# Walking the columns of ring weights and accumulators in interleaved halves or quarters

## Chip, cores and metric

The kernel runs on 1 core of one Trainium2 chip. The metric is the device time in microseconds; two runs of the kernel before took 2642.73 and 2643.3 us.

## What is computed

Two transformer blocks over 256 tokens of width 2048, batch 1, all in float32. The first has gated linear attention, forgetting attention and memory attention behind one input projection, an output projection and a squared-ReLU MLP of width 8192; the second has sparse attention, a pooling mixer, cross attention and a gated feed-forward layer of width 5632. By far most of the arithmetic is in the projections, of which this is the pattern:

```python
def first_block(x, ...):
    h = x
    xn = rms_norm(h, attn_norm_g)
    proj = xn @ w_in
    ...
    h = h + (o * gate) @ w_out
    u = jax.nn.relu(rms_norm(h, mlp_norm_g) @ w_up)
    h = h + (u * u) @ w_down
    return h

def second_block(x, ...):
    ...
    y = (jax.nn.silu(h @ w_gate[l]) * (h @ w_up[l])) @ w_down[l]
    x = x + rms_norm_2(y, ln_ffn_post[l])
    return x
```

## The kernel before

Every projection is cut into groups of 512 output columns. A group has two accumulators, one PSUM bank of 128x512 float32 for each half of the 256 tokens (`gb`, four banks in turn). It walks the 2048 or more input features 128 at a time.

Float32 accuracy comes from a split in two. A weight tile arrives by DMA as `raw` (five buffers, 128x1024, that is two feature tiles of 512 columns). ScalarE copies it to `wh`, rounded to the type in which TensorE takes a four-byte word per column in one pass (float32r; line 133 is the helper for every activation), and VectorE subtracts that from `raw` to get the rest, `wl` (line 366). The activations are split the same way into `H` and `L`. Each product is then three matmuls into the same bank: H by wh (line 460), H by wl (line 461), L by wh (line 462). The activations are the stationary operand (128x128), the weights the moving one (512 columns).

The pairs (`wh`, `wl`) form a ring of six slots. `split` takes the next free slot from the front of `self.ring`, and `run_groups` appends it at the back when its unit of work is done, so the slots come round in order. A few units at special places hold their pair in other buffers and have no slot (`un.slot` is None); two projections of 20 and 48 columns are computed the other way round, with the weights stationary and 256 token columns moving (lines 450 to 452).

Everything else, attention, norms and transposes, is cut into small tasks that `pump` slips in between the matmuls of a unit; their matmuls go through lines 197 and 203. TensorE's order is thus fixed when the program is built.

The gated linear attention has one place in which VectorE walks an operand in short runs. For levels 1 to 7, with s = 128 >> level (64, 32, ... 1), it picks runs of s words out of every 2s words, in products (line 158) of levels 4 to 7 (s = 8, 4, 2, 1) and in a predicated copy (line 833):

```python
dst = st.rearrange("p (x b w s) -> p x b w s", x=8, w=2, s=s)[:, :, :, 1]
self.nc.vector.copy_predicated(dst, mk, b.rearrange("p (x b s) -> p x b s", x=8, s=s))
```

## Time and profile before

| | |
|---|---|
| median of 2 runs | 2643.02 us (2642.73 to 2643.3) |
| profiled execution | 2642.02 us |
| its span, first to last instruction | 2640.3 us |
| mean granted TensorE clock | 0.998 |
| TensorE busy | 2616.5 us (99%) |
| VectorE busy | 1504.9 us (57%) |
| ScalarE busy | 1251.9 us (47%) |
| HBM traffic | 190 GB/s over the span |

The profile is of one execution. Busy time of TensorE is made of matmul durations that overlap their neighbours; what a matmul costs is the distance between two starts. "Idle before" is the time that an engine stood still ahead of a group of instructions, with what ended it.

### The profile page before, as it was taken

Reading aid. Unit: us, or ns where it says so; the run is one execution under the profiler, and the core shown is the slowest. Engines: PE = TensorE matmul, PEld = TensorE weight load, DVE = VectorE, ACT = ScalarE, POOL = GpSimd, SP = SyncE. Lnnn points to the kernel's source line nnn. Section 1 sums busy time; section 2 is a strip of 40 time slices with the busy share of each in tenths; the row PEclk is TensorE's granted clock in tenths of the full one; section 3 lists DMA queues with packets and bytes.
Section 4 is the critical chain, followed back from the end, with each engine's and each line's share of the span. In section 5 each row is a group of like instructions: output and inputs, shape, how many; then the busy total and the mean of one; then the engine's idle time right before and its main releaser. Section 6 shows DMA issues by size and latency. Waiting matters only on the chain.

```text
span 2640.3 us, 32053 instructions
## 1 busy us (share of the span) xinstructions
PE 2616.5 (99%) x12196; PEld 2168.9 (82%) x12196; DVE 1504.9 (57%) x1921; ACT 1251.9 (47%) x1708; POOL 76.5 (3%) x97
## 2 busy tenths in 40 slices
PE   9999999999999999999999999999999999999998
PEld 7888888888888888888888888888788888888886
DVE  6567655555555555555566545666755455555555
ACT  7544544444444444444455344465554444444443
POOL 0001000000000000001000000000100000000001
PEclk9999999999999999999999999999999999999999
DMA  9643565555566565555444557555455555556553
GB/s 343 204 139 119 166 216 185 188 188 184 191 201 223 187 223 195 191 202 198 150 143 147 190 177 258 201 199 184 136 193 189 192 188 194 186 195 202 195 186 129
DMA packets 138891, 500.18 MB, mean 189 GB/s; under 512 B 15650, under 2 KB 16594, under 8 KB 138737
## 3 DMA queue, kind: packets, MB, share of 16 engines
q1 hardware_dynamic: 131760, 473.16, 53.0%
q0 software_dynamic: 6976, 24.98, 2.7%
q8 instruction: 95, 1.56, 0.2%
q14 instruction: 60, 0.48, 0.1%
HBM read 493.33 MB, written 7.88 MB: 190 GB/s over the span
## 4 chain that ended last, share of the span: by engine, by line
PE 94%; issue 4%; DVE 1%; ACT 0%; DMA 0%; POOL 0%; SPq 0%; DVEq 0%; ACTq 0%; POOLq 0%
PE gb L460 29%; PE gb L462 29%; PE gb L461 29%; PE pb L197 4%; PE pb L203 3%; DVE wl L366 0%; DVE s L169 0%; DMA s<-memT 0%; DVE s L158 0%; POOL st L232 0%; ACT wh L133 0%; PE gb L451 0%; ACT s L133 0%; PE gb L450 0%; PE gb L452 0%
## 5 line engine op out<-in xcount | busy, mean ns | idle before, releaser
L366 DVE TENSOR_TENSOR wl<-raw,wh 128x1024 fp32r<-128x1024 f32 (+1 forms) x876 | 1052.8, 1219 | 689.5 <-ACT wh L133 687.4
L460 PE MATMUL gb<-wh,s 128*128 128x512 f32 x3496 | 1383.9, 396 | 2.2 <-ACT wh L133 2.1
L461 PE MATMUL gb<-wl,s 128*128 128x512 f32 x3496 | 1362.5, 390 | 2.5 <-DVE wl L366 2.5
L462 PE MATMUL gb<-wh,s 128*128 128x512 f32 x3496 | 1363.4, 390 | 0.0
L133 ACT ACTIVATE wh<-raw 128x1024 fp32r<-128x1024 f32 (+1 forms) x878 | 914.0, 1055 | 802.2 <-PE gb L462 766.8
L462 PEld LDWEIGHTS gb<-wh,s 128*128 128x128 f32 x3496 | 656.4, 188 | 139.3 <-DVE s L169 0.5
L460 PEld LDWEIGHTS gb<-wh,s 128*128 128x128 f32 x3496 | 657.2, 188 | 137.4 <-ACT wh L133 3.7
L461 PEld LDWEIGHTS gb<-wl,s 128*128 128x128 f32 x3496 | 657.5, 188 | 135.1 <-DVE wl L366 4.2
L158 DVE TENSOR_TENSOR s<-gb,s 128x512 f32<-128x512 f32 x144 | 98.1, 691 | 159.6 <-PE gb L462 130.5
L133 ACT ACTIVATE s<-pb 128x512 fp32r<-128x512 f32 (+4 forms) x171 | 89.4, 536 | 163.6 <-PE pb L203 139.5
L133 ACT ACTIVATE s<-gb,st 128x512 f32<-128x512 f32 (+1 forms) x112 | 70.0, 642 | 199.5 <-PE gb L462 188.0
L197 PE MATMUL pb<-s,s 128*128 128x128 f32 (+4 forms) x720 | 116.5, 301 | 1.3 <-DVE s L158 0.9
L203 PE MATMUL pb<-cc,s 128*128 128x128 f32 x700 | 106.0, 274 | 5.4 <-DVE s L169 5.3
L203 PEld LDWEIGHTS pb<-cc,s 128*128 128x128 f32 x700 | 87.0, 141 | 29.0 <-DVE s L169 6.6
L197 PEld LDWEIGHTS pb<-s,s 128*128 128x128 f32 x720 | 97.7, 191 | 9.5 <-DVE s L158 1.3
L158 DVE TENSOR_TENSOR s<-pb,s 128x512 fp32r<-128x512 f32 (+4 forms) x87 | 57.5, 664 | 62.4 <-ACT s L133 58.6
L133 ACT ACTIVATE s<-pb,vecs 128x256 fp32r<-128x256 f32 (+2 forms) x109 | 42.3, 453 | 49.9 <-PE pb L203 40.5
L163 DVE TENSOR_SCALAR s<-gb,st 128x512 f32<-128x512 f32 (+1 forms) x32 | 20.9, 658 | 67.8 <-PE gb L462 51.5
L169 DVE SCALAR_TENSOR_TENSOR s<-pb,vecs,s 128x256 fp32r<-128x256 f32 (+1 forms) x104 | 40.0, 435 | 29.0 <-ACT s L133 29.0
L133 ACT ACTIVATE s<-s,st 128x128 f32<-128x128 f32 (+2 forms) x73 | 32.8, 450 | 31.7 <-DVE st L163 30.4
L133 ACT ACTIVATE s<-s 128x512 f32<-128x512 f32 (+3 forms) x46 | 37.0, 807 | 21.5 <-DVE s L158 12.4
L232 POOL TENSOR_TENSOR st<-st,nhalf 128x8 f32<-128x8 f32 (+2 forms) x21 | 26.1, 1243 | 689.5 <-DVE st L165 689.5
(113 smaller groups left out, 565.0 us busy)
## 6 DMA issues: line engine op xcount, KB each, us to landing
raw<-w_in SPq DMA_DIRECT2D x216, 512.0 KB, 4.2
raw<-w_up SPq DMA_DIRECT2D x216, 512.0 KB, 4.4
raw<-w_down SPq DMA_DIRECT2D x216, 512.0 KB, 4.4
raw<-w_gate SPq DMA_DIRECT2D x88, 512.0 KB, 4.6
raw<-w_out SPq DMA_DIRECT2D x32, 512.0 KB, 4.5
raw<-w_mix_out SPq DMA_DIRECT2D x32, 512.0 KB, 4.6
raw<-w_br_pool SPq DMA_DIRECT2D x16, 512.0 KB, 5.2
raw<-w_br_attn SPq DMA_DIRECT2D x16, 512.0 KB, 4.1
```

Source lines behind the costliest of these rows:

```text
L133: self.nc.scalar.activation(out, in_, func, **kw)
L158: self.nc.vector.tensor_tensor(out, a, b, op)
L163: self.nc.vector.tensor_scalar(out, a, s1, None, op0=op0)
L169: self.nc.vector.scalar_tensor_tensor(out, a, s, b, op0, op1)
L197: self.nc.tensor.matmul(out, lhsT, rhs, start=start, stop=stop)
L203: self.nc.tensor.transpose(out, in_, self.ident[:k, :k])
L232: self.nc.gpsimd.tensor_tensor(r, t, self.nhalf[:, :k], op=OP.pow)
L366: self.nc.vector.tensor_sub(l[:, :m], r, h[:, :m].bitcast(F32))
L460: mm(o, H[:, c:c + 128], wh, start=st, stop=False)
L461: mm(o, H[:, c:c + 128], wl, start=False, stop=False)
L462: mm(o, L[:, c:c + 128], wh, start=False, stop=sp)
```

## The change

By ring slot, the moving operand (`wh` or `wl`) and the accumulator are both seen through the same rearranged view. `(a, c)` cuts the 512 columns into `a` parts and takes `c` columns of each in turn: (2, 2) takes columns 0, 1, 256, 257, 2, 3, 258, 259 and so on. The values and where they are summed stay the same; the order within a matmul changes. Slot 0 and the units without a slot keep the plain order.

```diff
@@ -454,9 +454,16 @@
                     if k % 4 == 3 and not sp:
                         self.pump()
                     continue
+                PAT = {0: None, 1: (2, 2), 2: (2, 4), 3: (2, 32), 4: (4, 2), 5: (2, 16)}[un.slot or 0]
+                if PAT:
+                    a_, c_ = PAT
+                    perm = lambda z: z.rearrange("p (a b c) -> p b a c", a=a_, c=c_)
+                else:
+                    perm = lambda z: z
+                wh, wl = perm(wh), perm(wl)
                 for t in ts:
                     c = (kt % 4) * 256 + t * 128
-                    o = g.bk[t]["ap"]
+                    o = perm(g.bk[t]["ap"])
                     mm(o, H[:, c:c + 128], wh, start=st, stop=False)
                     mm(o, H[:, c:c + 128], wl, start=False, stop=False)
                     mm(o, L[:, c:c + 128], wh, start=False, stop=sp)
```

On TensorE, in the first group of the program, this stands before for the second token half with ring slot 1 and then for slots 2 and 3 (`wh1`, `wl1` are slot 1's pair, `gb0` and `gb1` the accumulators of the token halves, `s` the split activations; the last column is the moving shape):

```order
L460 MATMUL gb1_83<-wh1_72,s2_3_133 128x512
L461 MATMUL gb1_83<-wl1_73,s2_3_133 128x512
L462 MATMUL gb1_83<-wh1_72,s3_4_134 128x512
L460 MATMUL gb0_82<-wh2_74,s2_3_133 128x512
L461 MATMUL gb0_82<-wl2_75,s2_3_133 128x512
L462 MATMUL gb0_82<-wh2_74,s3_4_134 128x512
L460 MATMUL gb1_83<-wh2_74,s2_3_133 128x512
L461 MATMUL gb1_83<-wl2_75,s2_3_133 128x512
L462 MATMUL gb1_83<-wh2_74,s3_4_134 128x512
L460 MATMUL gb0_82<-wh3_76,s2_3_133 128x512
```

and at the same place after (the three lines are 467 to 469 now; the shape reads partitions, jumps, parts, run):

```order
L467 MATMUL gb1_83<-wh1_72,s2_3_133 128x128x2x2
L468 MATMUL gb1_83<-wl1_73,s2_3_133 128x128x2x2
L469 MATMUL gb1_83<-wh1_72,s3_4_134 128x128x2x2
L467 MATMUL gb0_82<-wh2_74,s2_3_133 128x64x2x4
L468 MATMUL gb0_82<-wl2_75,s2_3_133 128x64x2x4
L469 MATMUL gb0_82<-wh2_74,s3_4_134 128x64x2x4
L467 MATMUL gb1_83<-wh2_74,s2_3_133 128x64x2x4
L468 MATMUL gb1_83<-wl2_75,s2_3_133 128x64x2x4
L469 MATMUL gb1_83<-wh2_74,s3_4_134 128x64x2x4
L467 MATMUL gb0_82<-wh3_76,s2_3_133 128x8x2x32
```

No row has moved: the operands and their order are the same, and only the shape in which the 512 columns are walked differs. A little later in the same group, still on TensorE, this stands after where the work goes from slot 4 to slot 5 (before, the same rows with 128x512):

```order
L467 MATMUL gb1_83<-wh4_78,s6_7_183 128x64x4x2
L468 MATMUL gb1_83<-wl4_79,s6_7_183 128x64x4x2
L469 MATMUL gb1_83<-wh4_78,s7_8_184 128x64x4x2
L467 MATMUL gb0_82<-wh5_80,s6_7_183 128x16x2x16
L468 MATMUL gb0_82<-wl5_81,s6_7_183 128x16x2x16
L469 MATMUL gb0_82<-wh5_80,s7_8_184 128x16x2x16
```

Slot 4 walks four quarters in runs of 2, slot 5 two halves in runs of 16; again nothing has moved.

## Rows read from the trace of the kernel before

**Rows 1.** The page, span and busy time of each engine

```profile
span 2640.3 us, 32053 instructions
...
PE 2616.5 (99%) x12196; PEld 2168.9 (82%) x12196; DVE 1504.9 (57%) x1921; ACT 1251.9 (47%) x1708; POOL 76.5 (3%) x97
```

**Rows 2.** The page, the chain that ended last, by engine and by line

```profile
PE 94%; issue 4%; DVE 1%; ACT 0%; DMA 0%; POOL 0%; SPq 0%; DVEq 0%; ACTq 0%; POOLq 0%
PE gb L460 29%; PE gb L462 29%; PE gb L461 29%; PE pb L197 4%; PE pb L203 3%; DVE wl L366 0%; DVE s L169 0%; DMA s<-memT 0%; DVE s L158 0%; POOL st L232 0%; ACT wh L133 0%; PE gb L451 0%; ACT s L133 0%; PE gb L450 0%; PE gb L452 0%
```

**Rows 3.** The page, costliest groups: count | busy us, mean ns | idle us, releaser

```profile
L366 DVE TENSOR_TENSOR wl<-raw,wh 128x1024 fp32r<-128x1024 f32 (+1 forms) x876 | 1052.8, 1219 | 689.5 <-ACT wh L133 687.4
L460 PE MATMUL gb<-wh,s 128*128 128x512 f32 x3496 | 1383.9, 396 | 2.2 <-ACT wh L133 2.1
L461 PE MATMUL gb<-wl,s 128*128 128x512 f32 x3496 | 1362.5, 390 | 2.5 <-DVE wl L366 2.5
L462 PE MATMUL gb<-wh,s 128*128 128x512 f32 x3496 | 1363.4, 390 | 0.0
L133 ACT ACTIVATE wh<-raw 128x1024 fp32r<-128x1024 f32 (+1 forms) x878 | 914.0, 1055 | 802.2 <-PE gb L462 766.8
```

**Rows 4.** Timeline of TensorE from 1000 to 1004 us: start, duration in us

```profile
999.82 0.39 PE L460 MATMUL gb<-wh,s 128*128 128x512 f32 x1
1000.05 0.39 PE L461 MATMUL gb<-wl,s 128*128 128x512 f32 x1
1000.28 0.39 PE L462 MATMUL gb<-wh,s 128*128 128x512 f32 x1
...
1003.90 0.39 PE L460 MATMUL gb<-wh,s 128*128 128x512 f32 x1
```

**Rows 5.** Engines' busy time in three long stretches, with granted clock

```profile
core 0: us, PE busy (x) PEld busy (x) DVE busy (x) ACT busy (x) POOL busy (x), PEclk, DMA share, GB/s
...
8.00:100.00 92.00, 89.54 (x400) 72.97 (x400) 59.65 (x76) 64.55 (x111) 9.12 (x10) 1.00 0.88 323
100.00:1900.00 1800.00, 1793.90 (x8534) 1489.64 (x8531) 1054.61 (x1446) 868.41 (x1234) 53.91 (x69) 1.00 0.55 185
1900.00:2626.00 726.00, 723.15 (x3236) 598.97 (x3237) 378.96 (x383) 311.56 (x351) 10.78 (x10) 1.00 0.56 186
```

**Rows 6.** Timeline of TensorE, 99.5 to 107 us, the 20-column projection

```profile
99.74 0.28 PE L450 MATMUL gb<-s,wh 128*20 128x256 f32 x1
99.86 0.28 PE L451 MATMUL gb<-s,wl 128*20 128x256 f32 x1
99.97 0.28 PE L452 MATMUL gb<-s,wh 128*20 128x256 f32 x1
...
102.37 0.28 PE L452 MATMUL gb<-s,wh 128*20 128x256 f32 x1
```

**Rows 7.** Timeline of VectorE, 163 to 178 us, levels 1 to 7 in order

```profile
163.44 0.73 DVE L833 COPY_PREDICATED s<-lmask,pb 128x512 f32<-128x512 int32 x1 [0.87 <-PE pb L197]
164.07 1.17 DVE L158 TENSOR_TENSOR s<-s,s 128x256 f32<-128x256 f32 x3
165.64 0.74 DVE L833 COPY_PREDICATED s<-lmask,pb 128x512 f32<-128x512 int32 x1 [0.40 <-PE pb L197]
166.27 1.17 DVE L158 TENSOR_TENSOR s<-s,s 128x256 f32<-128x256 f32 x3
...
168.61 0.71 DVE L833 COPY_PREDICATED s<-lmask,pb 128x512 f32<-128x512 int32 x1
169.22 1.17 DVE L158 TENSOR_TENSOR s<-s,s 128x256 f32<-128x256 f32 x3
170.42 0.72 DVE L833 COPY_PREDICATED s<-lmask,pb 128x512 f32<-128x512 int32 x1
171.04 1.17 DVE L158 TENSOR_TENSOR s<-s,s 128x256 f32<-128x256 f32 x3
...
173.38 0.70 DVE L833 COPY_PREDICATED s<-lmask,pb 128x512 f32<-128x512 int32 x1
174.71 1.31 DVE L833 COPY_PREDICATED s<-lmask,pb 128x512 f32<-128x512 int32 x1 [0.63 <-PE pb L197]
...
176.99 1.30 DVE L833 COPY_PREDICATED s<-lmask,pb 128x512 f32<-128x512 int32 x1
```

## The prediction

> **What bounds the kernel now.** I read the engine totals first: TensorE is busy 2616.5 of 2640.3 us, the next engine, VectorE, 1504.9 [rows 1]. The chain that ended last confirms that it is the limit: 94% of it is TensorE, 29% on each of lines 460, 461 and 462 [rows 2]. The costliest groups give the counts: each of these three lines has 3496 matmuls of 512 columns against weights from the ring, 10488 in all, and they sat idle for only about 2 us each; the ScalarE split that feeds them was idle 802.2 us, 766.8 of it waiting for line 462, that is, for TensorE to let go of a ring slot [rows 3]. So a nanosecond on each of these matmuls is 10.5 us of the end, and nothing that the change does elsewhere can count.

> The mean duration in those rows (390 to 396 ns) is not the price of a matmul, since they overlap. The price is the distance from one start to the next: in a quiet stretch of the timeline 18 steps take 1003.90 - 999.82 = 4.08 us, 226.7 ns each [rows 4]. [...] It isn't a fixed cost of a matmul: those of 256 columns on lines 450 to 452, with only 20 columns of stationary operand to load, take 23 steps in 102.37 - 99.74 = 2.63 us, 114.3 ns each, again about 0.445 ns a column [rows 6]. [...]

> **What the change does.** No instruction is added, removed or moved: the same matmuls stand in the same order on TensorE, and the other engines' work is the same. Only the access patterns of lines 460 to 462 differ, by ring slot. The ring is first in, first out over six slots, so each slot has a sixth of the matmuls, about 1748. Slot 0 and the units outside the ring keep their order. Slots 1 to 5 walk weights and accumulator in runs of 2, 4, 32, 2 and 16 words, from two halves 1024 bytes apart (slots 1, 2, 3, 5) or four quarters 512 bytes apart (slot 4). No new wait appears; LDWEIGHTS, the splits and the transfers are untouched.

> What a run of two costs on TensorE this trace doesn't show: no matmul of it walks so. The nearest rows are on VectorE, in the gated linear attention, where one operand is walked in runs of 64, 32, ... 1 words with gaps of the same length. The predicated copy (line 833) of 512 words takes 0.73, 0.74, 0.71, 0.72 and 0.70 us for runs of 64, 32, 16, 8 and 4, and then 1.31 and 1.30 us for runs of 2 and 1 [rows 7]. Runs of 4 every 8 words cost nothing; runs of 2 every 4 words cost 1.87 times as much, and so do single words every 2: in both, 512 words lie spread over 256 aligned groups of four words, and in the earlier ones over 128. So what that operation pays for is groups of four touched, not words and not jumps. On the other side, three products on line 158 take 1.17 us together whether the runs are 8, 4, 2 or 1 [rows 7]: at VectorE's pace of about a word per nanosecond a pair per group is still no burden. TensorE asks for a word every 0.44 ns, more than twice that pace, and with pairs it would have to open a new group every 0.89 ns, twice as often as it does now.

> The sum, slot by slot:
> - Slots 2, 3 and 5 (runs of 4, 32, 16; all begin on a group's first word): still 128 groups for each matmul. I cost them at nothing, because runs of 4 and more are free in both VectorE rows. [...]
> - Slots 1 and 4 (runs of 2): every pair opens a group, and the other half of the group is fetched again later: 256 groups. [...] Upper bound: the predicated copy's extra 0.61 us for its 256 pairs, laid on each matmul as it stands. In between, 256 groups at TensorE's own 1.77 ns are 453.4 ns, and the copy's ratio of 1.87 gives 424 ns. I take 453.4, since it is priced by TensorE's own row, and 424 is near.
> - So 2 x 1748 = 3496 matmuls cost 226.7 ns more each: +792.5 us.
> - What the slower matmuls hide: TensorE stood idle for 2.5, 6.1 and 2.9 us in the three long stretches [rows 5], mostly on splits and transfers. Splits will now be ready earlier relative to TensorE, so up to some 11 us could go; I take 6.
> - Accumulators: they are walked in the same order, so sums land where they did. A write in pairs I cost at nothing more than the fetch, as the two go in step.

> The profiled execution took 2642.02 us (its span 2640.3), 1.0 below the median of 2643.02. From the median: 2643 + 792.5 - 6 = about 3429 us. With 424 ns in place of 453.4 it is 3327; with both halves of the cost a little dearer, up to 3530. Its own range is 3320 to 3530.

> [...]

> **The rivals.**
> - *Pairs are free* (ends at no change). If SBUF hands TensorE two adjacent words per access whatever the jump between accesses, all five orders run at 226.7 ns and the time stays at 2643. For it: line 158's 1.17 us with runs of 2 and 1, and every run in the change being even and aligned. Against it: the predicated copy, which doubled with the same runs. [...]
> - *Two groups can be held open.* Then the two halves of slot 1 share their fetches and are free, and only the four quarters of slot 4 pay: 1748 x 226.7 = 396 us, 3036 with 3 us hidden. A price for both slots well under double (say 50% more, 3496 x 113 = +395) ends at the same place. Nothing in the trace speaks for either beyond the two VectorE rows disagreeing.
> - *Every jump costs a group's time*, slot 2's included: three slots double, 5244 x 226.7 = +1189, about 3825; the upper bound of the pair price, 3496 x 0.61 = +2130, lies beyond. Against it: runs of 4 cost nothing in either row.
> [...]

> **How the numbers follow.** Forecast 0.48; pairs free 0.26; one slot or a part of the price 0.14; every jump dear 0.05; faster 0.07. The prediction is 3429 us. For 8 in 10 the range must hold the first three: 2635 to 3530, which leaves out 0.07 below and about 0.06 above. Slower by over 2% is 0.48 + 0.14 + 0.05 = 0.67, within 2% 0.26, faster by over 2% 0.07; 2% is about what a measurement of this kernel tells from no change.

> **What would show it.** In the profile after, the distances between starts of the three matmul lines should fall into two kinds by shape: about 453 ns for the shapes of 128x2x2 and 64x4x2, and 227 ns for all others. TensorE's busy share stays at 99%, ScalarE's and VectorE's fall to about 0.37 and 0.44 of the span, with their added idle time put down to line 462's successor. I am wrong if 128x2x2 runs at 227 (pairs free, or held open, according to what 64x4x2 does), if 64x2x4 is slower than 8x2x32, or if any shape comes under 220.

## The result and the profile after

The changed kernel took 3295.93 us (median of 2 runs, 3294.96 to 3296.89) against 2643.02: a ratio of 1.2471, 95% interval 1.2449 to 1.2492. It is slower by 653 us, where 786 were forecast, most of it in the two slots from which the forecast had its cost (table below). The profiled execution took 3294.96 us with a span of 3293.2, 652.9 more than before.

The page, span, engines and the chain that ended last, to be read beside [rows 1, 2]:

```profile
span 3293.2 us, 32051 instructions
...
PE 3274.3 (99%) x12196; PEld 2230.0 (68%) x12196; DVE 1510.1 (46%) x1921; ACT 1263.4 (38%) x1708; POOL 76.6 (2%) x97
...
PE 99%; DVE 0%; ACT 0%; DMA 0%; SPq 0%; issue 0%; POOL 0%; DVEq 0%; ACTq 0%
PE gb L467 31%; PE gb L468 31%; PE gb L469 31%; PE pb L197 3%; PE pb L203 2%; DMA s<-memT 0%; DVE wl L366 0%; DVE s L169 0%; ACT s L133 0%; PE gb L452 0%; PE gb L451 0%; PE gb L450 0%; ACT wh L133 0%; SPq L340 0%; SPq L208 0%
```

The number of matmuls is the same, 12196, VectorE's and ScalarE's work is the same to 1%, and TensorE alone has grown, by 658 us of busy time. The costliest groups, to be read beside [rows 3]:

```profile
L467 PE MATMUL gb<-wh,s 128*128 128x512 f32 x3496 | 1627.9, 466 | 1.4 <-ACT wh L133 1.3
L468 PE MATMUL gb<-wl,s 128*128 128x512 f32 x3496 | 1605.6, 459 | 1.2 <-DVE wl L366 1.2
L469 PE MATMUL gb<-wh,s 128*128 128x512 f32 x3496 | 1605.4, 459 | 0.0
L366 DVE TENSOR_TENSOR wl<-raw,wh 128x1024 fp32r<-128x1024 f32 (+1 forms) x876 | 1055.3, 1219 | 1055.7 <-ACT wh L133 1048.1
L133 ACT ACTIVATE wh<-raw 128x1024 fp32r<-128x1024 f32 (+1 forms) x878 | 922.5, 1063 | 1212.9 <-PE gb L469 1162.0
```

All three lines grew by 242 to 244 us of busy time, whichever operand they stream, and the split on ScalarE now waits 1162.0 us for line 469 where it waited 766.8 for line 462, the same matmul. A group of the profile mixes the six slots, so the price of an order has to be read from starts in the timeline. The first matmuls of six units in a row, on slots 1, 2, 3, 4, 5 and 0, each unit of 12 matmuls (start, duration in us):

```profile
1904.57 0.68 PE L467 MATMUL gb<-wh,s 128*128 128x512 f32 x1
...
1908.68 0.42 PE L467 MATMUL gb<-wh,s 128*128 128x512 f32 x1
...
1911.69 0.40 PE L467 MATMUL gb<-wh,s 128*128 128x512 f32 x1
...
1914.54 0.68 PE L467 MATMUL gb<-wh,s 128*128 128x512 f32 x1
...
1919.91 0.43 PE L467 MATMUL gb<-wh,s 128*128 128x512 f32 x1
...
1922.83 0.40 PE L467 MATMUL gb<-wh,s 128*128 128x512 f32 x1
...
1925.59 0.50 PE L467 MATMUL gb<-wh,s 128*128 128x512 f32 x1
```

A twelfth of each distance is 343, 251, 238, 448, 243 and 230 ns; before, all were at 227 [rows 4]. Over the whole trace, taking each matmul's start to the next matmul's start and sorting by the ring slot of its weights (the sums include what waits fell there):

| slot, order | matmuls | median ns, before | after | sum us, before | after | more | forecast |
|---|---|---|---|---|---|---|---|
| 0, plain | 1758 | 227 | 229 | 404.7 | 408.8 | 4.1 | 0 |
| 1, (2, 2) | 1746 | 227 | 340 | 407.0 | 597.8 | 190.8 | 396 |
| 2, (2, 4) | 1746 | 227 | 254 | 401.6 | 442.0 | 40.4 | 0 |
| 3, (2, 32) | 1746 | 227 | 236 | 403.9 | 418.6 | 14.7 | 0 |
| 4, (4, 2) | 1740 | 227 | 443 | 400.3 | 777.1 | 376.8 | 396 |
| 5, (2, 16) | 1752 | 227 | 240 | 403.8 | 429.5 | 25.7 | 0 |

The sum, 652.5 us, is the whole difference of the spans. Nothing went anywhere else.

### The profile page after: what moved, and what is told of

Read it like the earlier page. It is cut to its first block, busy times and chain, and to the rows that moved or that the text cites. A ratio compares the mean times of both kernels' runs of the same rounds, so it can differ in the third digit from the quotient of the medians.

```text
span 3293.2 us, 32051 instructions
## 1 busy us (share of the span) xinstructions
PE 3274.3 (99%) x12196; PEld 2230.0 (68%) x12196; DVE 1510.1 (46%) x1921; ACT 1263.4 (38%) x1708; POOL 76.6 (2%) x97
## 4 chain that ended last, share of the span: by engine, by line
PE 99%; DVE 0%; ACT 0%; DMA 0%; SPq 0%; issue 0%; POOL 0%; DVEq 0%; ACTq 0%
PE gb L467 31%; PE gb L468 31%; PE gb L469 31%; PE pb L197 3%; PE pb L203 2%; DMA s<-memT 0%; DVE wl L366 0%; DVE s L169 0%; ACT s L133 0%; PE gb L452 0%; PE gb L451 0%; PE gb L450 0%; ACT wh L133 0%; SPq L340 0%; SPq L208 0%
## 5 line engine op out<-in xcount | busy, mean ns | idle before, releaser
L467 PE MATMUL gb<-wh,s 128*128 128x512 f32 x3496 | 1627.9, 466 | 1.4 <-ACT wh L133 1.3
L468 PE MATMUL gb<-wl,s 128*128 128x512 f32 x3496 | 1605.6, 459 | 1.2 <-DVE wl L366 1.2
L469 PE MATMUL gb<-wh,s 128*128 128x512 f32 x3496 | 1605.4, 459 | 0.0
L133 ACT ACTIVATE wh<-raw 128x1024 fp32r<-128x1024 f32 (+1 forms) x878 | 922.5, 1063 | 1212.9 <-PE gb L469 1162.0
L469 PEld LDWEIGHTS gb<-wh,s 128*128 128x128 f32 x3496 | 676.4, 193 | 341.1 <-issue 143.2
L467 PEld LDWEIGHTS gb<-wh,s 128*128 128x128 f32 x3496 | 676.4, 193 | 322.0 <-issue 130.0
L468 PEld LDWEIGHTS gb<-wl,s 128*128 128x128 f32 x3496 | 676.2, 193 | 317.5 <-issue 127.4
L158 DVE TENSOR_TENSOR s<-gb,s 128x512 f32<-128x512 f32 x144 | 99.0, 691 | 267.5 <-PE gb L469 226.7
L203 PEld LDWEIGHTS pb<-cc,s 128*128 128x128 f32 x700 | 89.5, 144 | 44.3 <-issue 18.9
```

The lines of the kernel that those rows point to most:

```text
L133: self.nc.scalar.activation(out, in_, func, **kw)
L158: self.nc.vector.tensor_tensor(out, a, b, op)
L203: self.nc.tensor.transpose(out, in_, self.ident[:k, :k])
L467: mm(o, H[:, c:c + 128], wh, start=st, stop=False)
L468: mm(o, H[:, c:c + 128], wl, start=False, stop=False)
L469: mm(o, L[:, c:c + 128], wh, start=False, stop=sp)
```

## The experiments

Kernels for which one time is given ran once; the kernel before, run seven times beside the first four kernels below, took 2641.13 to 2643.95 us (median 2643.28). Each edit is against the changed kernel or, where said, against the kernel before. The three matmul lines shift by a few with each edit. Medians are of the distances from one start to the next, by slot, as in the table.

**Which side pays, the read or the write.** Two kernels, each with one half of the change: the first permutes only the weights, the second only the accumulators.

```diff
-                    o = perm(g.bk[t]["ap"])
+                    o = g.bk[t]["ap"]
```

> Only the weights are walked in the new orders, the accumulators plainly, so columns of slots 1 to 5 are summed into the wrong places (the values differ, the number and size of all instructions do not). SBUF theory (the moving read pays for groups of words that it opens): all of the cost is here, start distances of 340 ns (128x2x2) and 443 ns (64x4x2) as in the changed kernel, time 3280 to 3300 us. PSUM theory (the accumulator write pays): every matmul at 227 ns, time 2640 to 2650 us. Both pay and add up: a time between, 2800 to 3150 us, with the rest in the run that permutes the accumulators alone.

```diff
-                wh, wl = perm(wh), perm(wl)
```

> Only the accumulators are walked in the new orders, the weights plainly; the values land in other columns, the work is the same. SBUF theory: 2640 to 2650 us, 227 ns for all slots. PSUM theory: 3280 to 3300 us, with 340 and 443 ns. Both pay: between.

With the weights alone permuted the time was 3295.36 us, the changed kernel's within 0.6 us, and the medians by slot were 340, 254, 236, 443 and 240 ns, the same as in the table. With the accumulators alone it was 2643.74 us, the kernel before's (2643.28), and 227 ns in every slot. The first matmul line of the kernel that permutes the weights, to be read beside the changed kernel's:

```profile
L467 PE MATMUL gb<-wh,s 128*128 128x512 f32 x3496 | 1627.6, 466 | 2.1 <-ACT wh L133 2.1
```

The costliest groups of the kernel that permutes the accumulators, the same as [rows 3]:

```profile
L466 PE MATMUL gb<-wh,s 128*128 128x512 f32 x3496 | 1384.0, 396 | 2.8 <-ACT wh L133 2.7
L467 PE MATMUL gb<-wl,s 128*128 128x512 f32 x3496 | 1363.1, 390 | 2.6 <-DVE wl L366 2.5
L468 PE MATMUL gb<-wh,s 128*128 128x512 f32 x3496 | 1363.8, 390 | 0.0
```

So the whole cost is in reading the moving operand from SBUF; the order of the writes into PSUM cost nothing in any of the five patterns.

**The change without its pairs.** Slots 1 and 4 plain, the others as changed:

```diff
-                PAT = {0: None, 1: (2, 2), 2: (2, 4), 3: (2, 32), 4: (4, 2), 5: (2, 16)}[un.slot or 0]
+                PAT = {0: None, 1: None, 2: (2, 4), 3: (2, 32), 4: None, 5: (2, 16)}[un.slot or 0]
```

> Slots 1 and 4, which walked in runs of two, go back to the plain order; slots 2, 3 and 5 keep (2,4), (2,32) and (2,16). If each slot's matmuls pay for their own order alone, what is left is 39 + 16 + 25 us (the slot sums of the changed kernel less those of before): 2715 to 2730 us, 2.7 to 3.3% slower than before. Rival, as the prediction had it: runs of four and more are free, and their small extra in the changed kernel came from their neighbours in pairs: 2640 to 2655 us.

It took 2727.59 us (median of 4 runs) against 2643.28, a ratio of 1.0319 (1.0302 to 1.0336). Line 467 of its page:

```profile
L467 PE MATMUL gb<-wh,s 128*128 128x512 f32 x3496 | 1413.1, 404 | 2.0 <-ACT wh L133 1.9
```

Its sums by slot are 41 us more in slot 2, 16 in slot 3 and 22 in slot 5, much as in the changed kernel: 79 us for three slots, and 5 us more in slot 0, which has kept the plain order. Each order pays for itself, and the price of longer runs is real, where the prediction had nothing.

**More streams.** Weights and accumulators together, other numbers in slots 1 to 5:

```diff
-                PAT = {0: None, 1: (2, 2), 2: (2, 4), 3: (2, 32), 4: (4, 2), 5: (2, 16)}[un.slot or 0]
+                PAT = {0: None, 1: (8, 2), 2: (4, 4), 3: (8, 4), 4: (2, 8), 5: (4, 16)}[un.slot or 0]
```

> Weights and accumulators in the same order, with other numbers for slots 1 to 5: (8,2), (4,4), (8,4), (2,8), (4,16). Group theory (with more than two streams every pair opens its group of four words anew at some 1.73 ns, and runs of four are whole groups): (8,2) at 443 ns as (4,2); (4,4), (8,4), (2,8), (4,16) between 227 and 255 ns; time about 3120 us. Distance theory (what costs is the 512 bytes between quarters, less so the 1024 between halves): (8,2), with 256 bytes between its parts, is well away from 443 ns, and (4,4) is dearer than the 254 ns of (2,4), at 300 ns or more.

3295.73 us, where the group theory gave about 3120; that it is nearly the changed kernel's time is chance, since the slots differ. The medians were 487 ns for (8, 2), 269 for (4, 4), 278 for (8, 4), 244 for (2, 8) and 232 for (4, 16). This separates little: eight streams of pairs cost 10% more than the group theory's 443, (4, 4) lies above its 255, but not at the 300 of the distance theory. Distance and number of streams changed together here, so the next kernel parts them.

**Distance or streams.** Moving read alone, pairs, with the parts at chosen distances (against the kernel before; distances in words of four bytes):

```diff
+                W = {1: (2, 128), 2: (2, 512), 3: (2, 32), 4: (4, 256), 5: (4, 64)}.get(un.slot) if un.nkt == 2 else None
+                if W:
+                    m_, d_ = W
+
+                    def walk(z):
+                        return bass.AP(z.tensor, z.offset, [list(z.ap[0]), [2, 256 // m_], [d_, m_], [1, 2]])
+                    wh, wl = walk(h), walk(l)
```

> Moving read alone, pairs only, accumulators plain (the weights read are other columns, some twice, so the values differ; number and size of the instructions are the same). Two streams 512, 2048 and 128 bytes apart in slots 1, 2 and 3, four streams 1024 and 256 bytes apart in slots 4 and 5. Stream theory (the port can keep two groups open, not four): 340 ns in slots 1 to 3 and 443 ns in slots 4 and 5 whatever the distance, time about 3990 us. Distance theory (how far a jump goes sets its price, 512 bytes being dear and 1024 cheap): slot 1 at 443 ns or more, slot 4 at 340, slot 2 at 340 or less.

3968.61 us; medians 340, 340 and 327 ns for two streams, 443 and 443 for four. The timeline at the first matmuls of slots 2, 3, 4, 5 and 0, where four streams 1024 bytes apart (the third row to the fourth) take the same 5.32 us for twelve as four streams 256 bytes apart (the fourth row to the fifth):

```profile
2292.64 0.51 PE L467 MATMUL gb<-wh,s 128*128 128x512 f32 x1
...
2296.58 0.51 PE L467 MATMUL gb<-wh,s 128*128 128x512 f32 x1
...
2300.52 0.64 PE L467 MATMUL gb<-wh,s 128*128 128x512 f32 x1
...
2305.84 0.64 PE L467 MATMUL gb<-wh,s 128*128 128x512 f32 x1
...
2311.16 0.43 PE L467 MATMUL gb<-wh,s 128*128 128x512 f32 x1
```

The distance theory falls: for pairs in streams like these, what counts is how many streams are alternated, not how far apart they are.

**Groups opened, or jumps.** One ascending stream, moving read alone (against the kernel before); each list is [step, count], innermost last, and a step of 0 reads the same words again:

```diff
+                steps = {1: [[4, 256], [1, 2]], 2: [[2, 128], [0, 2], [1, 2]], 3: [[8, 128], [1, 4]],
+                         4: [[4, 64], [0, 2], [1, 4]], 5: [[16, 16], [0, 2], [1, 16]]}.get(un.slot) if un.nkt == 2 else None
+                if steps:
+                    walk = lambda z: bass.AP(z.tensor, z.offset, [list(z.ap[0])] + steps)
+                    wh, wl = walk(h), walk(l)
```

> Moving read alone, one ascending stream, accumulators plain (other columns are read, some twice; number and size of the instructions are the same). Slot 1: pairs every 4 words (256 groups of four, each opened once); slot 2: every pair read twice running (64 groups); slot 3: four words every 8 (128 groups); slot 4: every four words read twice running (64 groups); slot 5: every 16 words read twice running (64 groups, opened twice). [...] Jump theory (each access that does not follow on the last costs, whether or not its group is open): 340 ns in slots 1 and 2 alike, 227 to 255 in slots 3 and 4, 240 in slot 5.

3028.04 us. The first matmuls of slots 2, 3, 4, 5, 0 and 1 and of the unit behind:

```profile
1757.18 0.40 PE L465 MATMUL gb<-wh,s 128*128 128x512 f32 x1
...
1759.79 0.40 PE L465 MATMUL gb<-wh,s 128*128 128x512 f32 x1
...
1762.59 0.38 PE L465 MATMUL gb<-wh,s 128*128 128x512 f32 x1
...
1765.18 0.41 PE L465 MATMUL gb<-wh,s 128*128 128x512 f32 x1
...
1768.06 0.40 PE L465 MATMUL gb<-wh,s 128*128 128x512 f32 x1
...
1770.83 0.61 PE L465 MATMUL gb<-wh,s 128*128 128x512 f32 x1
...
1776.25 0.40 PE L465 MATMUL gb<-wh,s 128*128 128x512 f32 x1
```

A twelfth each: 218, 233, 216, 240, 231 and 452 ns; the medians over the trace are 216, 233, 216, 240, 231 and 452. Pairs that each open a new group cost 452; pairs that are each read twice running cost 216. The second walk has half as many jumps as the first (128 steps back for 255 steps on), so the two are not quite alike, but it is also faster than the plain order, which has none. The jump theory wanted 340 for both and falls; in slot 5 it had the right number, 240. The group theory (the price is the number of groups opened) holds: 256 groups at 1.77 ns are 453.4. And with only 64 groups to open, a matmul runs at 216 ns, below the 227 of the kernel before.

**Aligned groups, or length of run.** Moving read alone again (against the kernel before), a start and the steps:

```diff
+                walk = {1: (2, [[8, 128], [1, 4]]), 2: (0, [[4, 128], [512, 2], [1, 2]]), 3: (0, [[2, 128], [514, 2], [1, 2]]),
+                        4: (0, [[2, 512]]), 5: (2, [[16, 64], [1, 8]])}.get(un.slot) if un.nkt == 2 else None
+                if walk:
+                    at, steps = walk
+                    wh, wl = [bass.AP(z.tensor, z.offset + at, [list(z.ap[0])] + steps) for z in (h, l)]
```

> Moving read alone, accumulators plain (other columns are read, so the values differ; number and size of the instructions are the same). Slot 1: four words of every eight, beginning on the third word of a group, so that each run lies across two groups (256 groups); slot 2: two streams 2048 bytes apart, each taking a pair of every group once (256 groups, none returned to); slot 3: two streams in pairs as in the change, but half a group out of step with each other; slot 4: every second word alone (256 groups, two words of each); slot 5: eight words of every sixteen, beginning on the third word (three groups to a run, 192 in all). Group theory (1.77 ns for each aligned group of four words opened): 453 ns in slots 1, 2 and 4, and 340 ns in slot 5; slot 3 stays at 340 if the half price of two streams does not hang on their being in step. Run-length theory (runs of four and more words are nearly free wherever they begin, shorter ones dear): 233 ns in slot 1, 240 in slot 5, 443 to 453 in slot 2 and more than that, towards 900, in slot 4.

4246.3 us; medians 452, 487, 330, 451 and 330 ns for slots 1 to 5. The first matmuls of slots 2, 3, 4, 5, 0 and 1 and of the unit behind:

```profile
2450.99 0.67 PE L465 MATMUL gb<-wh,s 128*128 128x512 f32 x1
...
2456.90 0.51 PE L465 MATMUL gb<-wh,s 128*128 128x512 f32 x1
...
2460.86 0.63 PE L465 MATMUL gb<-wh,s 128*128 128x512 f32 x1
...
2466.27 0.51 PE L465 MATMUL gb<-wh,s 128*128 128x512 f32 x1
...
2470.20 0.40 PE L465 MATMUL gb<-wh,s 128*128 128x512 f32 x1
...
2472.96 0.61 PE L465 MATMUL gb<-wh,s 128*128 128x512 f32 x1
...
2478.38 0.68 PE L465 MATMUL gb<-wh,s 128*128 128x512 f32 x1
```

Runs of four that begin two words later than in the kernel before it, and so touch two groups, go from 233 to 452 ns (5.42 us for the twelve of slot 1). Single words, two to a group, cost 451, no more than pairs. Three groups to eight words, 192 in all, cost 330, or 1.72 ns each. The run-length theory falls. One number misses: two streams of pairs that never return to a group cost 487, not 453, so alternating adds 34 ns of its own. Beside slot 2 of the kernel with chosen distances, two streams of pairs at the same 2048 bytes that do return to each group, for 340 ns, it also shows that a group returned to is cheaper than a new one.

## Why the prediction was right, and where its sizes were off

The prediction looked for two kinds of start distance, about 453 and 227 ns. The slots show one for each order, with medians from 229 to 443 ns.

*What bounds the kernel* held: the sum over the three matmul lines is the whole difference, and every other engine only waits longer.

*The step on which all hung* is the price in the sum, "256 groups at TensorE's own 1.77 ns". It is the 226.7 ns of a plain matmul over its 128 groups [rows 4]; that the time goes by groups and not by columns was the author's estimate, with a doubtful analogy on VectorE, and no row of the kernel before shows it on TensorE. That the analogy pointed the right way was in part luck: on line 833 only the destination is walked in runs, and TensorE reads its weights, while line 158, whose sources are walked in runs, had pairs free. (The pace there is also 1.5 ns a word, three products of 256 words in 1.17 us, and 1.2 on line 366 [rows 3], not about one.) The runs show the price for one ascending stream: 451 or 452 ns for 256 groups whether they are opened by pairs, single words or straddling fours, 330 for 192, 227 for the 128 of the plain order, and 216 where 64 are enough. At 64 something else sets the time, since 64 groups at 1.77 ns would be 113.

*Slot 4* was forecast at 453.4 ns and came at 443: 376.8 us for 396.

*Slot 1* is the mis-sized term: "the other half of the group is fetched again later: 256 groups", 396 us, of which 190.8 came. At 340 ns two streams pay as for 192 groups, as if half the returns to a group were free. The second rival, two groups held open, had slot 1 free and slot 4 paying; for slot 1 the truth lies midway between it and the forecast, and half as much again, which that rival also named for both slots, fits slot 1 alone. That returning is what comes cheaper is shown: two streams of pairs 2048 bytes apart cost 340 ns where they return to each group and 487 where they return to none. That it is the number of streams is shown (two at any of four distances cost 327 to 340, four at any of three 443); why exactly half is left open, and that the two streams are in step is not the reason, since half a group out of step cost 330.

*Slots 2, 3 and 5* were costed "at nothing, because runs of 4 and more are free in both VectorE rows". Those rows walk one ascending stream with gaps, and the change takes its runs in turn from two halves. On TensorE the walk of those rows is nearly free too: four words of every eight cost 233 ns, 6 above plain, in the kernel that counts groups, while runs of four from two halves cost 254. So the step that failed is to have taken a walk with gaps for one that alternates; why alternating costs is not shown. The three slots cost 40.4, 14.7 and 25.7 us, 81 in all, and 79 in the kernel without pairs. The named sign of error, 64x2x4 slower than 8x2x32, did appear.

*The accumulators* at nothing: shown, by the kernel that permutes them alone.

*What the slower matmuls hide*, 6 us: TensorE's idle time went from 23.8 (2640.3 - 2616.5) to 18.9 us (3293.2 - 3274.3), 4.9 hidden.

So the forecast had 205 us too much in slot 1 and 19 in slot 4, 81 too little in slots 2, 3 and 5 and 4 in slot 0, and took off 6 us for hidden idle time that the sums by slot already hold; together these are the 133 us between 3429 and 3296. That the sum came nearer than its terms is luck, since too much and too little partly cancel. The time lies 24 us below the forecast's own range, 3320 to 3530.

*Pairs are free*, the main rival, fell: pairs that each open a new group cost 452 ns against the plain order's 227, at a mean granted clock of 0.998 in both runs.

*Faster*, which had a chance of 0.07, fell too: no order of 512 different words that was tried came under the plain order's 227 ns in the median.

## What to carry to other kernels

## What the hardware showed that was not expected

Even the plain order pays for its groups: with 64 groups opened in place of 128, each pair or each four read twice running, a matmul of 512 columns took 216 ns, against 226.7. That is 10.7 ns on 10488 matmuls, some 112 us or 4% of the kernel before, which no order tried here gets back. Alternating between streams has a price of its own beyond groups: 9, 13, 17 and 27 ns more than plain at runs of 32, 16, 8 and 4 from two halves, 269 and 278 ns for runs of 4 from four and eight parts, 487 for eight streams of pairs. But runs of 16 cost less from four parts (232) than from two (240), and one stream that reads every 16 words twice running also costs 240. A rule for these was not found.
